# Hybrid GLA, window-attention and PEER block on one core: 19 instead of 14 experts' up-products done beside the gate layout

## The chip, the core and the metric

The kernel is one layer of a diffusion backbone, run on one NeuronCore of a Trainium2 chip. The metric is the device time of the whole kernel in microseconds (us), median over runs. Five engines work side by side, each through its own instructions in the order written: PE (matmuls), DVE (vector), ACT (scalar, activation functions), POOL (GpSimd) and SP, which here only issues transfers. Transfers run on DMA queues and are issued by SP, by ACT (the writes of the gate layout) and by POOL (the gathers).

## What is computed

The first half of the layer (modulation, projections, gated linear attention, window attention, output projection, layer norm) makes a stream `x1` of 1024 tokens. The second half, where the change lies, retrieves for each token 8 heads x 16 of 16384 single-neuron experts:

```python
def _peer(h, peer_wq, peer_subkeys, peer_u, peer_v):
    ...
        top_s, pos = lax.top_k(cand, PEER_TOPK)
        eidx = jnp.take_along_axis(cidx, pos, axis=-1)
        gate = jax.nn.softmax(top_s, axis=-1)
        u = peer_u[eidx]
        v = peer_v[eidx]
        act = jax.nn.gelu(jnp.einsum('pd,phkd->phk', xt, u).astype(jnp.float32), approximate=False)
        return jnp.einsum('phk,phkd->pd', (gate * act).astype(v.dtype), v)
```

All is float32. The kernel gets close to float32 from the faster matmul format by splitting each operand into a high and a low part and adding three products (`mm3`, lines 113 to 117).

## The kernel before, in words

The 1024 tokens are 8 tiles of 128. Five of them (`ND = 5`) go the **dense** way: all 16384 experts are computed for these 640 tokens, and a mostly empty gate matrix selects. Three (`NS = 3`) go the **sparse** way: for each of 3 x 128 (tile, rank) steps one gather fetches the 128 tokens' expert rows (`uv`, 1 MB), DVE makes the dot product, ACT the Gelu, and the weighted value rows are added.

The 16384 experts are 128 rows of 128. The text calls one such row, `jj` = 0 to 127, "an expert" as the change does. One expert's **up-product** (`products`, line 901) is: two loads of 256 KB (`uraw`), their split into `uhi` (ACT) and `ulo` (POOL or DVE), and two halves of 24 matmuls of 128x320 into PSUM (`pact`), 48 matmuls in all. Its **gating** (`gated`, line 1071) is Gelu, times the gate, and a split into `W`. Its **output** (`outputs`, line 1105) multiplies `W` with the value rows; experts go in pairs (`JG = 2`), and each pair ends in ten additions to `yacc` on DVE (line 1120). While the outputs of one pair are computed, the up-products of the next pair are woven in.

The order of the program is this:

- The **gate layout** (`gates`, line 779). For each dense tile it turns the retrieved expert numbers and gates into a matrix `g_d` in DRAM. It goes in 160 steps of four tokens: DVE makes two one-hot tiles (`oa`, line 824, and `wb`, line 810), ACT scales four of them (`ob`, line 828), PE multiplies (`pgb`, line 832), ACT copies the result out (`gstage`, line 834). Every eighth step ACT issues a write to `g_d`.
- Beside its later part run the last pair's retrieval (`rest`), the first 20 sparse steps (`first`), and the up-products of some experts ahead of time (`early`, the table `EARLY`). An early expert's product goes to DRAM (`act_d`, lines 1042 and 1043) and is read back by `gated` when its turn comes. There `ulo` is made by POOL (line 111).
- The **dense stage** then goes over `jj` = 0 to 127. For an expert in `EARLY` it loads `gearly` (160 KB a half) in place of computing the products; for the others it computes them, and makes `ulo` on DVE (line 900). The rest of the sparse steps are spread over it: `advance` counts 0.25 for each half of a product and 0.1 for each of the ten outputs of a pair, and asks for so many sparse steps by the share done.
- At the end come the last pair's outputs and the last layer norm.

Parts that run side by side are interleaved by `weave`, which gives each part a number of steps and a share of the stretch. The lines are:

```python
weave((made, GLEFT, *SPANS[0]), (rest(), 34, *SPANS[1]), (early(), 2 * len(EARLY), *SPANS[2]), (first(), FIRST, *SPANS[3]))
...
made = None if jj in EARLY or jj in filled else products(jj, ep, pe, (7, 2, 2))
```

After `weave` a scheduler still moves instructions of one engine past each other where data allow, so the built order of each engine is what counts. It is shown with the change.

Of the kernel before, what the change touches and what calls it, by code (L numbers as in the profile page):

```python
# [37 lines left out]
def kernel(ctx: ExitStack, tc: tile.TileContext, A, out):  # L38
# [49 lines left out]
    g_d = drm.tile([TD // GT, 128, 128, GT], F32, name="g_d")  # L88
    act_d = [drm.tile([128, TD], F32, name=f"act_d{j}") for j in range(len(EARLY))]

# [4 lines left out]
    def weave(*parts):  # L95

        parts = [(g, n, *(at or (0, 1))) for g, n, *at in parts]
        order = sorted((a + (s + 0.5) / n * (b - a), i) for i, (_, n, a, b) in enumerate(parts) for s in range(n))
        for _, i in order:
            next(parts[i][0], None)  # L100
        for g, *_ in parts:
            for _ in g:
                pass
# [798 lines left out]
    def products(jj, ub, pb, bufs):  # L902

        u = []
        for c in range(2):
            raw = ub.tile([128, 4, 128], F32, tag="raw", name="uraw", bufs=bufs[0])
            nc.sync.dma_start(raw, A["ut"][jj, :, 4 * c:4 * c + 4, :])
            hi = ub.tile([128, 4, 128], F32R, name="uhi", bufs=bufs[1])
            lo = ub.tile([128, 4, 128], F32R, name="ulo", bufs=bufs[1])
            if pb is ps:  # L910
                split(hi, lo, raw, G)
            else:
                apart(hi, lo, raw, "u")
            u.append((hi, lo))
        for h in range(2):
            p = pb.tile([128, 512], F32, tag="trp", name="pact", bufs=bufs[2])
            for k in range(KC):
                mm3(p[:, :HW], [x[:, k % 4, :] for x in u[k // 4]], [x[:, k, HW * h:HW * h + HW] for x in hhD], k, KC)
            yield h, p[:, :HW]
# [115 lines left out]
    with ExitStack() as gx:  # L1035
        ue = pool(gx, "ue", side="right")

        def early():
            for i, jj in enumerate(EARLY):
                for h, p in products(jj, ue, ps, (3, 2, 2)):  # L1040
                    ga = ue.tile([128, HW], F32, name="gact", bufs=2)
                    S.activation(ga, p, AF.Copy)
                    nc.sync.dma_start(act_d[i][:, HW * h:HW * h + HW], ga)
                    yield
# [3 lines left out]
        def first():  # L1048

            for _ in range(FIRST):  # L1050
                next(steps)
                done[0] += 1
                yield

        done = [0]
        def rest():

            yield from after
            retrieved.append(True)

        weave((made, GLEFT, *SPANS[0]), (rest(), 34, *SPANS[1]), (early(), 2 * len(EARLY), *SPANS[2]), (first(), FIRST, *SPANS[3]))
    px.close()
# [9 lines left out]
    def gated(jj, h):  # L1072
# [7 lines left out]
        w = wts[jj]  # L1080
        if jj in EARLY:
            src = ep.tile([128, HW], F32, name="gearly", bufs=2)
            nc.sync.dma_start(src, act_d[EARLY.index(jj)][:, HW * h:HW * h + HW])
        else:
            src = acts.pop((jj, h))
        if jj in EARLY or jj in filled:
            ga = pe.tile([128, 512], F32, tag="trp", name="gact", bufs=2)[:, :HW]
# [86 lines left out]
PICK = 1.3  # L1174
GATE = 1
GLEFT = 152
SPANS = ((0, 1), (0, 0.6), (0.5, 1), (0.2, 0.8))
EARLY = [0, 1, 2, 3] + list(range(12, 128, 12))
UB = 3
BATCH = 2  # L1180
FIRST = 20
# [124 lines left out]
```

## Time and profile before

| what | value |
|---|---|
| time, median of 3 runs | 3144.02 us (3141.66 to 3146.41) |
| the profiled execution's own time | 3149.91 us |
| its span, first to last instruction | 3148.1 us |
| mean granted TensorE clock | 0.948 |
| gate layout, first `gstage` to last | 857.8 to about 1316 us |
| first early product's matmul | 999.0 us |
| last early product's matmul | 1229.6 us |
| first matmul of an output (`pyd`) | 1344.4 us |
| last product's split (`W`) | about 3086 us |

How to read it: busy times of engines overlap, and their sum is no time. In a row of a group "mean ns of one" is the time of one instruction; matmuls are pipelined, so the time from the start of one to the start of the next is shorter than that. The share of each engine over the whole span mixes stages with different limits, so each stage is read by itself.

### The profile page before, as it was taken

The numbers are of one execution on the slowest core, as the hardware profiler recorded it, in microseconds if no ns is written. First come the engines' busy times: TensorE is split into PE (matmuls) and PEld (weight loads), VectorE is DVE, ScalarE is ACT, GpSimd is POOL, SyncE is SP. The second block draws the span as 40 slices with busy tenths as digits, with TensorE's granted clock in tenths as the row PEclk, the third lists the DMA queues.
The fourth block names the chain that finished last, engine by engine and source line by source line (L and its number), as shares of the span: only waits on it lengthen the run. The fifth ranks groups of instructions, "written<-read, shape, count | busy, mean of one in ns | idle before, by whom it ended". The sixth has DMA issues, their size and how long they took to land. (4 is left out here: it accounts for less than half of the span.)

```text
span 3148.1 us, 49158 instructions
## 1 busy us (share of the span) xinstructions
PE 2829.2 (90%) x16604; PEld 2449.8 (78%) x16604; DVE 2349.6 (75%) x5684; ACT 1837.6 (58%) x3947; POOL 1609.1 (51%) x1111
## 2 busy tenths in 40 slices
PE   6998878888778887889999999999999999999994
PEld 3687856767568787768888888888988888989993
DVE  4318844578798999478788877777777778787878
ACT  3324544443546778766666666666666666666673
POOL 0012301043443544137667666767667677777775
PEclk8999879989889999999999999999999999999997
DMA  9653665646466566678799998888988989898983
GB/s 329 222 185 123 211 228 201 211 166 201 153 231 224 218 221 255 254 237 321 288 321 336 335 329 302 314 312 312 345 304 308 324 323 342 330 338 324 340 323 144
DMA packets 352680, 848.82 MB, mean 270 GB/s; under 512 B 27627, under 2 KB 165611, under 8 KB 299692
## 3 DMA queue, kind: packets, MB, share of 16 engines
q1 hardware_dynamic: 285520, 384.20, 37.1%
q0 software_dynamic: 55296, 402.68, 33.6%
q10 hardware_dynamic: 11612, 58.81, 4.8%
q8 instruction: 131, 2.15, 0.3%
q14 instruction: 121, 0.99, 0.1%
HBM read 745.43 MB, written 100.16 MB: 269 GB/s over the span
## 5 line engine op out<-in xcount | busy, mean ns | idle before, releaser
L1023 POOL TENSOR_TENSOR ys<-ys,uv 128x1024 f32<-128x1024 f32 x362 | 870.2, 2404 | 454.0 <-ACT uv L1022 421.2
L117 PE MATMUL pact<-hhD,ulo 128*128 128x320 f32 x2048 | 639.9, 314 | 15.3 <-POOL ulo L111 14.3
L115 PE MATMUL pact<-hhD,uhi 128*128 128x320 f32 x2048 | 641.9, 314 | 10.9 <-DVE W L111 8.2
L116 PE MATMUL pact<-hhD,uhi 128*128 128x320 f32 x2048 | 639.1, 312 | 0.0
L115 PE MATMUL pyd<-vhi,W 128*128 128x512 f32 x1280 | 505.5, 402 | 32.8 <-DVE yacc L1120 22.6
L116 PE MATMUL pyd<-vlo,W 128*128 128x512 f32 x1280 | 508.0, 397 | 18.0 <-DVE vlo L900 17.8
L117 PE MATMUL pyd<-vhi,W 128*128 128x512 f32 x1280 | 506.1, 397 | 0.0
L1120 DVE TENSOR_TENSOR yacc<-yacc,pyd 128x512 f32<-128x512 f32 x630 | 418.6, 681 | 101.1 <-PE pyd L117 100.0
L989 POOL DMA_INDIRECT uv<-in_uv_dram,ex x384 | 375.1, 977 | 222.3 <-issue 53.6
L1006 DVE SCALAR_TENSOR_TENSOR uv<-uv,h2p 128x1024 f32<-128x1024 f32 x384 | 464.1, 1212 | 17.1 <-DMA uv<-in_uv_dram,ex 15.9
L117 PEld LDWEIGHTS pact<-hhD,ulo 128*128 128x128 f32 x2048 | 390.2, 191 | 30.6 <-POOL ulo L111 15.9
L115 PEld LDWEIGHTS pact<-hhD,uhi 128*128 128x128 f32 x2048 | 390.5, 191 | 29.9 <-DVE W L111 10.0
L1022 ACT ACTIVATE uv<-uv,w 128x1024 f32<-128x1024 f32 x362 | 395.3, 1140 | 29.6 <-DVE w L1011 14.3
L116 PEld LDWEIGHTS pact<-hhD,uhi 128*128 128x128 f32 x2048 | 390.5, 191 | 11.7
L115 PEld LDWEIGHTS pyd<-vhi,W 128*128 128x128 f32 x1280 | 242.2, 190 | 86.8 <-DVE yacc L1120 33.3
L116 PEld LDWEIGHTS pyd<-vlo,W 128*128 128x128 f32 x1280 | 243.5, 190 | 60.3 <-DVE vlo L900 20.9
L117 PEld LDWEIGHTS pyd<-vhi,W 128*128 128x128 f32 x1280 | 243.3, 190 | 53.9 <-DVE W L111 0.6
L832 PE MATMUL pgb<-ob,oa 128*128 128x128 f32 x1280 | 196.0, 300 | 56.0 <-ACT ob L828 37.2
L900 DVE TENSOR_TENSOR vlo<-pv,vhi 128x512 fp32r<-128x512 f32 x256 | 175.7, 686 | 93.6 <-ACT pv L899 92.9
L895 ACT ACTIVATE vhi<-vraw 128x512 fp32r<-128x512 f32 x256 | 157.7, 625 | 140.2 <-DMA vraw<-in_uv_dram 94.0
L832 PEld LDWEIGHTS pgb<-ob,oa 128*128 128x128 f32 x1280 | 179.6, 204 | 69.3 <-ACT ob L828 55.7
L828 ACT ACTIVATE ob<-wb,gj 128x128 f32<-128x128 bf16 x640 | 209.5, 409 | 10.6 <-DVE wb L810 7.8
(357 smaller groups left out, 5378.0 us busy)
## 6 DMA issues: line engine op xcount, KB each, us to landing
uraw<-in_ut_dram SPq DMA_DIRECT2D x256, 256.0 KB, 6.7
vraw<-in_uv_dram SPq DMA_DIRECT2D x256, 256.0 KB, 6.8
g_d<-gstage ACTq DMA_DIRECT2D x20, 2048.0 KB, 6.7
gload<-g_d SPq DMA_DIRECT2D x32, 1280.0 KB, 13.8
wo<-wo_d SPq DMA_DIRECT2D x64, 512.0 KB, 5.9
wq<-wq_d SPq DMA_DIRECT2D x64, 512.0 KB, 6.3
wt<-in_w_ada_dram SPq DMA_DIRECT2D x48, 512.0 KB, 5.4
wq_d<-wqs SPq DMA_DIRECT2D x16, 512.0 KB, 6.3
```

The costliest lines, as they stand in the source:

```text
L115: PE.matmul(out_, l[0], r[0], start=(k == 0), stop=False)
L116: PE.matmul(out_, l[0], r[1], start=False, stop=False)
L117: PE.matmul(out_, l[1], r[0], start=False, stop=(k == n - 1))
L828: S.activation(o[1][:, c], w[:, :, c], AF.Copy, scale=gj[:, q + c:q + c + 1])
L832: PE.matmul(p[:, c::4], o[0][:, h + c], o[1][:, h + c], start=True, stop=True)
L895: S.activation(hi, src, AF.Copy)
L900: V.tensor_tensor(lo, p, hi.bitcast(F32), OP.subtract)
L989: G.indirect_dma_start(out=uv[n][0].rearrange("p a d -> p (a d)"), out_offset=None, in_=A["uv"], in_offset=bass.IndirectOffsetOnAxis(ap=ch ...
L1006: pin(V.scalar_tensor_tensor(t[:, 0], t[:, 0], 1.0, h2[j], OP.mult, OP.mult, accum_out=w[:, i:i + 1]))
L1022: S.activation(v, v, AF.Copy, scale=wb)
L1023: G.tensor_tensor(ys[j], ys[j], v, OP.add)
L1120: V.tensor_tensor(ya, ya, p, OP.add)
```

## The change

`EARLY` names 19 experts in place of 14, every eighth from 8 on in place of every twelfth from 12 on, and the early products' share of the woven stretch begins at 0.35 in place of 0.5:

```diff
-SPANS = ((0, 1), (0, 0.6), (0.5, 1), (0.2, 0.8))
-EARLY = [0, 1, 2, 3] + list(range(12, 128, 12))
+SPANS = ((0, 1), (0, 0.6), (0.35, 1), (0.2, 0.8))
+EARLY = [0, 1, 2, 3] + list(range(8, 128, 8))
```

So five experts' products (240 matmuls, 10 loads, 10 `uhi`, 10 `ulo`) leave the dense stage and stand beside the gate layout, with 10 copies `gact` and 10 writes `act_d` more there, and 10 loads `gearly` more in the dense stage. In the dense stage their `ulo` was on DVE, with a copy `pu` on ACT; beside the gate layout it is on POOL.

On **PE**, at the end of the gate layout. `pgb` are the gate layout's matmuls, `pact` those of the up-products. Up to the first of these rows both kernels have the same order of PE from the first `pgb` on. Before:

```order
L116 MATMUL pact<-hhD_10355,uhi 128x320
L117 MATMUL pact<-hhD_10354,ulo 128x320
L832 MATMUL pgb<-ob,oa 128x128 x186
L115 MATMUL pact<-hhD_10354,uhi 128x320
L116 MATMUL pact<-hhD_10355,uhi 128x320
L115 MATMUL pact<-hhD_10354,uhi 128x320
```

Now, a piece of the same stretch and its end:

```order
L832 MATMUL pgb<-ob,oa 128x128 x5
L117 MATMUL pact<-hhD_10359,ulo 128x320
L832 MATMUL pgb<-ob,oa 128x128 x5
L115 MATMUL pact<-hhD_10359,uhi 128x320
L832 MATMUL pgb<-ob,oa 128x128
L116 MATMUL pact<-hhD_10360,uhi 128x320
L832 MATMUL pgb<-ob,oa 128x128 x2
```

```order
L832 MATMUL pgb<-ob,oa 128x128
L116 MATMUL pact<-hhD_10360,uhi 128x320
L117 MATMUL pact<-hhD_10359,ulo 128x320
L832 MATMUL pgb<-ob,oa 128x128 x48
L115 MATMUL pact<-hhD_10359,uhi 128x320
```

The 186 `pgb` that stood alone now have all 240 added `pact` among their first 138; the last 48 stand alone. The `pact` behind the last `pgb` are those of the dense stage's first experts in both.

On **ACT**, in the same stretch (`uhi` and `gact` belong to early products, `w` to a sparse step, the rest to the gate layout). Before:

```order
L1010 ACTIVATE w<-w 128x1
L828 ACTIVATE ob<-wb,gj 128x128 x16
L1010 ACTIVATE w<-w 128x1
L834 ACTIVATE gstage<-pgb 128x128x4
L828 ACTIVATE ob<-wb,gj 128x128 x4
L834 ACTIVATE gstage<-pgb 128x128x4
```

Now:

```order
L1042 ACTIVATE gact<-pact 128x320
L828 ACTIVATE ob<-wb,gj 128x128 x13
L1010 ACTIVATE w<-w 128x1
L828 ACTIVATE ob<-wb,gj 128x128 x3
L1042 ACTIVATE gact<-pact 128x320
L110 ACTIVATE uhi<-uraw 128x512
L834 ACTIVATE gstage<-pgb 128x128x4
L828 ACTIVATE ob<-wb,gj 128x128 x4
```

The ten `uhi` and ten `gact` stand between the gate layout's steps, some right beside the sparse steps' `w`.

On **POOL**, from the last early `ulo` on (`uv` are the gathers). Before:

```order
L735 TENSOR_TENSOR oh<-ohb,ce 128x800 x2
L111 TENSOR_TENSOR ulo<-uraw,uhi 128x512
L735 TENSOR_TENSOR oh<-ohb,ce 128x800
L111 TENSOR_TENSOR ulo<-uraw,uhi 128x512
L989 DMA uv<-in_uv_dram,ex_10021 128x2048 x11
L1023 TENSOR_TENSOR ys<-ys,uv 128x1024 x2
```

Now:

```order
L989 DMA uv<-in_uv_dram,ex_10026 128x2048 x2
L111 TENSOR_TENSOR ulo<-uraw,uhi 128x512 x2
L989 DMA uv<-in_uv_dram,ex_10026 128x2048
L111 TENSOR_TENSOR ulo<-uraw,uhi 128x512
...
L989 DMA uv<-in_uv_dram,ex_10026 128x2048
L111 TENSOR_TENSOR ulo<-uraw,uhi 128x512 x3
L989 DMA uv<-in_uv_dram,ex_10026 128x2048 x3
L1023 TENSOR_TENSOR ys<-ys,uv 128x1024 x2
```

Eight of the eleven gathers now have the ten added `ulo` among and behind them. DVE's instructions in this stretch are the same in number and kind.

## Rows read from the trace of the kernel before

**Rows 1.** Busy share in 40 slices of the span, PE, granted clock, DMA.
```profile
PE   6998878888778887889999999999999999999994
PEclk8999879989889999999999999999999999999997
DMA  9653665646466566678799998888988989898983
```
**Rows 2.** Windows, busy us (instructions) by engine, then clock, DMA share, GB/s.
```profile
1100.00:1225.00 125.00, 104.42 (x726) 101.17 (x725) 120.00 (x233) 100.12 (x285) 61.83 (x53) 0.93 0.59 220
1229.60:1316.50 86.90, 61.94 (x374) 55.16 (x372) 60.05 (x110) 75.40 (x226) 14.73 (x9) 0.92 0.64 250
```
**Rows 3.** Timeline of ACT: start us, us, line, operation, count.
```profile
1299.31 0.60 ACT L834 ACTIVATE gstage<-pgb 128x512 f32<-128x512 f32 x1
1299.79 1.31 ACT L828 ACTIVATE ob<-wb,gj 128x128 f32<-128x128 bf16 x4
1300.99 0.60 ACT L834 ACTIVATE gstage<-pgb 128x512 f32<-128x512 f32 x1
```
**Rows 4.** Waits of ACT, 1229.6 to 1316.5: total us, times, longest.
```profile
ACT w L1010 <- DVE uv L1006: 11.1, 2, 5.7
```
**Rows 5.** Groups of ACT by line, 1000 to 1230: busy us, mean ns, idle before.
```profile
L110 ACT ACTIVATE uhi<-uraw 128x512 fp32r<-128x512 f32 x27 | 16.8, 630 | 3.5 <-PE pact L116 1.9 <-issue 1.5
L1042 ACT ACTIVATE gact<-pact 128x320 f32<-128x320 f32 x28 | 12.0, 434 | 11.9 <-PE pact L117 11.9
```
**Rows 6.** Timeline of PE, `pact` back to back at full clock.
```profile
1325.80 0.31 PE L117 MATMUL pact<-hhD,ulo 128*128 128x320 f32 x1
...
1326.97 0.31 PE L116 MATMUL pact<-hhD,uhi 128*128 128x320 f32 x1
```
**Rows 7.** Windows cut at every tenth `yacc` addition: pairs with one early expert.
```profile
1805.84:1831.86 26.02, 24.04 (x128) 20.70 (x127) 20.54 (x37) 14.25 (x26) 18.85 (x13) 1.00 0.99 362
1980.21:2007.86 27.65, 23.99 (x127) 20.80 (x127) 19.01 (x35) 14.02 (x27) 19.24 (x12) 1.00 0.86 316
2151.45:2178.70 27.25, 24.79 (x124) 21.28 (x123) 19.07 (x37) 14.84 (x27) 17.44 (x11) 0.94 0.92 338
...
2661.99:2682.48 20.49, 20.49 (x112) 18.21 (x111) 17.59 (x34) 13.36 (x23) 13.74 (x9) 1.00 1.03 377
...
sum 234.79, PE 225.97 PEld 198.99 DVE 190.28 ACT 141.02 POOL 158.32; mean PE 22.60 PEld 19.90 DVE 19.03 ACT 14.10 POOL 15.83
```
**Rows 8.** The same cut: the 50 other pairs from 1406.46 to 3061.
```profile
sum 1446.13, PE 1410.31 PEld 1258.92 DVE 1126.13 ACT 954.95 POOL 1032.36; mean PE 28.21 PEld 25.18 DVE 22.52 ACT 19.10 POOL 20.65
```
**Rows 9.** Waits of PE in the dense stage, 1400 to 3084.
```profile
PE pyd L116 <- DVE vlo L900: 17.8, 7, 5.3
PE pyd L115 <- DVE yacc L1120: 16.8, 16, 2.6
PE pact L115 <- DVE W L111: 8.2, 5, 4.5
```
**Rows 10.** Waits of POOL, 1229.6 to 1275.
```profile
POOL uv L989 <- DVE ys L1020: 39.9, 8, 12.1
```
**Rows 11.** Groups of DVE by line, 1100 to 1225.
```profile
L824 DVE TENSOR_TENSOR oa<-iotab,f 128x512 f32<-128x512 bf16 x46 | 37.5, 824 | 0.0
L810 DVE TENSOR_TENSOR wb<-wide,f 128x512 bf16<-128x512 bf16 x47 | 31.0, 666 | 0.0
```
**Rows 12.** The same groups, 1270 to 1316.
```profile
L824 DVE TENSOR_TENSOR oa<-iotab,f 128x512 f32<-128x512 bf16 x26 | 17.9, 690 | 4.1 <-PE pgb L832 2.0
L810 DVE TENSOR_TENSOR wb<-wide,f 128x512 bf16<-128x512 bf16 x22 | 9.3, 424 | 7.9 <-ACT ob L828 7.9
```
**Rows 13.** Groups of POOL by line, 1000 to 1240.
```profile
L111 POOL TENSOR_TENSOR ulo<-uraw,uhi 128x512 fp32r<-128x512 f32 x28 | 39.7, 1425 | 44.4 <-DMA g_d<-gstage 30.1 <-ACT uhi L110 14.2
```
**Rows 14.** DMA issues: count, KB each, median us to landing.
```profile
uraw<-in_ut_dram SPq DMA_DIRECT2D x256, 256.0 KB, 6.7
```

## The prediction, made before the changed kernel was run

> **What bounds the kernel now.** I read the 40 slices first, then windows by stage, then the waits and the timeline of the two stretches that the change touches. The slices [rows 1] show two regimes: from the seventeenth slice on PE is busy at nine tenths at full clock, with DMA at eight or nine tenths; before it PE is at seven or eight. The dense stage is PE's. There PE waits in all for some 43 us of 1684, mostly for DVE: `vlo` late 17.8, `yacc` late 16.8, `W` late 8.2 [rows 9].
>
> The gate layout has two parts. While the retrieval runs beside it (1100 to 1225) DVE is busy 120 of 125 us and is the bound [rows 2]. After the last early product, from 1229.6 to 1316.5, DVE falls to 60 of 86.9 us and ACT is the longest, 75.4 us; it loses 11.1 us more to two waits for a sparse step's dot product, whose gather had not landed [rows 2, 4]. Without these waits a step takes 1.68 us on ACT (four `ob` and one `gstage`, from 1299.31 to 1300.99) [rows 3]. I call this stretch of 86.9 us the tail. PE is busy 61.9 us in it [rows 2], spread out by the waits for `ob`. The built order puts all 240 added matmuls into the tail, and moves nothing ahead of it, although the woven share starts earlier: so the stretch in which DVE is 96% busy keeps its length, and the sum has two terms, the tail and the dense stage.
>
> **The dense stage.** What goes is 5 x 48 matmuls. Back to back at full clock one starts 0.146 us after the other (eight starts in 1.17 us) [rows 6], so an expert is 7.0 us of PE and five are 35.1 us. That is the upper end. The better measure is the pair of experts, since it holds what DVE and DMA take back. Cut at every tenth addition to `yacc`, ten pairs with one early expert took 234.8 us, 23.5 each, and 50 other pairs 1446.1 us, 28.9 each [rows 7, 8]. One product less therefore saved 5.4 us, not 7.0. Five make **27.2 us**; I take this, because the change makes five more of just this kind of pair. What the 1.6 us are: an early pair keeps its ten additions, its `W` and its `vlo`, so DVE is at 190.3 of 234.8 us (81%) against 1126.1 of 1446.1 (78%) [rows 7, 8], and PE catches up with it. With the products ten loads of 256 KB go and ten of 160 KB come; `uhi` and `pu` on ACT and `ulo` on DVE go too. None of these ends last, so I count them at nothing; the cover is PE itself. The sparse steps are paced by the work done, so the same number lies in a shorter stage, about 1.6% denser; the cost of that is in the pair measure only as far as the early pairs already show it. The bound from below is taken from the three worst early pairs, 26.0, 27.7 and 27.3 us [rows 7]: 28.9 less their mean of 27.0 is 1.95, five make 9.8 us.
>
> **The tail.** It gets 240 matmuls on PE (35.1 us), ten `uhi` and ten `gact` on ACT, ten `ulo` on POOL, and on SP ten loads and ten writes.
> - ACT: ten `uhi` and ten `gact` at the busy time of one here, 16.8/27 and 12.0/28 us, are 6.2 + 4.3 = 10.5 us [rows 5]. ACT is the bound, so this is added. Each `gact` also waits for PE's last matmul: 11.9 us over 28 so far [rows 5], ten make 4.3 us. Together **14.8 us**.
> - PE: 61.9 + 35.1 = 97 us must fit into 86.9 + 14.8 = 101.7. It does, with little to spare, and the 61.9 include matmuls drawn out by waits [rows 2], so PE should not end later than ACT. If nothing overlapped, the tail would grow by the full 35.1.
> - POOL: 14.7 us busy [rows 2], plus ten `ulo` at 1.425 us, 14.3 [rows 13]. It has room. But POOL works in order, and eight gathers stand among the `ulo`; see the first rival.
> - SP: the last `act_d` write is now ahead of the six loads for the dense stage's first products. By the built order 32 `ob`, eight steps of 1.68 us or 13.4 us, come after the last `gact`; a load lands in 6.7 us [rows 14]. So I count it at nothing, with 6.7 us to spare.
> - Bounds: below, nothing, if the twenty short ACT instructions fill the 11.1 us in which ACT waits [rows 4]; above, POOL's waits of 39.9 us (first rival). I take 14.8 because ACT's queue is in order: a `gact` behind a waiting `w` waits with it.
>
> DVE's two one-hot instructions show what a busy POOL does beside it: `oa` takes 824 ns and `wb` 666 while POOL is at 61.8 of 125 us, and 690 and 424 when POOL stands still [rows 2, 11, 12]. A step is so 0.376 us dearer for DVE. In the tail POOL would be at 29 of 101.7 us: 46.5 steps x 0.376 x (0.285/0.495) = 10.1 us more on DVE, which has 26.9 us free. I count it at nothing, and it is a rival below. The Trainium skill, "SBUF — State Buffer", section on the two separate sides, states it more sharply: DVE and GpSimd share a port pair as an exclusive lock, and whoever comes second is fully blocked for the whole instruction. The slower `oa` and `wb` agree with that; by this rule all ten `ulo` could stand in DVE's way, 14.3 us by their duration here, and the sum would come to +1.9.
>
> **Sum.** -27.2 + 14.8 = **-12.4 us**. The profiled execution took 3149.9, so its like would take 3137.5; it lies 5.9 above the median of the runs, so I forecast a median of **3131.6 us**. Alone this case reaches from about 3122 to 3140 (tail 8 to 22, dense 22 to 33).
>
> **The rivals.**
> 1. *POOL's gathers hold the added products: slower.* A `ulo` behind a gather waits for whatever the gather waits for: a free buffer, which DVE's `ys` of an older sparse step gives. Over 1229.6 to 1275 POOL waited so 39.9 us in eight waits, the longest 12.1 [rows 10]. If these reach PE through `ulo`, the `pgb` queued behind on PE stand too, and with them ACT's `gstage`. The tail grows by 39.9: -27.2 + 39.9 = +12.7, **3156.7**. It decides from the point where the tail grows by more than 27.2. For it: seven of ten `ulo` stand before the last of the eight gathers. Against it: the eight gathers were all issued by 1275, 45 us into the tail [rows 10], and in the built order 102 of the 186 `pgb` stand ahead of the products of the last three `ulo`; these are 25.5 steps, 43 us at ACT's pace alone. So it is close, but mostly in step. Chance 0.13.
> 2. *The dense stage gives little back.* The stage is already near its transfers' limit: the shortest early pair ran at 377 GB/s and a DMA share of 1.03 [rows 7]. If the added early pairs are like the three worst, 9.8 us come back: +5.0, **3149**. Against it: the ten took 234.8 us, so the other seven average 22.0 [rows 7]. Chance 0.16.
> 3. *The tail swallows the work.* ACT's added 14.8 fill its 11.1 us of waits: +3.7, and -23.5 in all, **3120.5**; with the full 35.1 of the dense stage 3112.6. For it: PE and POOL have room in these waits; against it the order. Chance 0.11.
> 4. *POOL's `ulo` hold DVE, and DVE becomes the tail's bound.* The 10.1 us come on top: -2.3, **3141.7**. Against it are DVE's 26.9 free us. Chance 0.08.
>
> That the change does nothing is no rival: the order shows the 240 matmuls moved.
>
> **Numbers.** My forecast has 0.52. A measurement of this kernel tells 0.2%, 6.3 us, from no change. Faster: 0.42 of the forecast, rival 3, and a little of rival 4: 0.55. Same: 0.10 of the forecast, rival 4, and half of rival 2: 0.25. Slower: rival 1 and the rest of rival 2: 0.20. The range reaches down to rival 3 with the upper bound of the dense stage, and up to most of rival 1: 3113 to 3154; about 0.15 is left out.
>
> **What would show it.** In the profile of the changed kernel: the last `gstage` some 15 us later than 1316, with the first early product still near 999; in the tail ACT still the busiest, near 86 us; `pgb` waiting mainly for `ob`. In the dense stage fifteen early pairs of about 23.5 us, the others at 28.9, and first `pyd` to last some 27 us shorter. If the last `gstage` comes 30 us or more later and PE waits for `ulo` in the tail, rival 1 is right; if early pairs take 26 us or more, or other pairs grow beyond 29.5, rival 2; if the last `gstage` moves less than 6 us, rival 3; if DVE's idle time in the tail is gone and `pgb` waits for `oa`, rival 4. The forecast is wrong if the tail grows by more than 25 us or the dense stage shrinks by less than 18.

## The result: faster by 44 us, with the profile after

| what | before | after |
|---|---|---|
| median of 4 runs (us) | 3144.92 (3141.66 to 3146.41) | 3101.21 (3094.94 to 3112.23) |
| profiled execution's own time, span | 3149.91, 3148.1 | 3094.94, 3093.2 |
| first `pact` / last `gstage` | 999.0 / 1315.8 | 1002.1 / 1325.1 |
| first `pyd` / last `pyd` | 1344.4 / 3105.6 | 1355.9 / 3033.2 |
| last `pyd` to the end | 42.5 | 59.9 |

The ratio is 0.9856, 95% interval 0.9833 to 0.9879. The forecast was 3131.6 (3113 to 3154): the sign held, the size did not. The two profiled executions differ by 54.9 us: the first `pyd` comes 11.5 later, the dense stage is **83.9 shorter** (forecast 27.2), and the end **17.4 longer** (forecast nothing).

**The tail.** The window of the changed kernel that answers to the second of [rows 2], from the last product of the fourteenth early expert to the end of the gate layout:

```profile
1233.20:1326.70 93.50, 84.55 (x614) 80.35 (x613) 65.84 (x109) 84.87 (x247) 25.45 (x20) 1.00 0.71 270
```

Waits of ACT in it, against [rows 4] (total us, times, longest):

```profile
ACT gstage L834 <- PE pgb L832: 2.4, 4, 1.0
ACT uhi L110 <- PE pact L116: 2.4, 2, 1.4
ACT uhi L110 <- DMA uraw<-in_ut_dram: 2.1, 1, 2.1
ACT w L1010 <- DVE uv L1006: 0.6, 1, 0.6
...
ACT gact L1042 <- ACT w L1010: 0.3, 1, 0.3
```

Waits of POOL in it, against [rows 10]:

```profile
POOL uv L989 <- DVE ys L1020: 21.4, 6, 7.7
POOL ulo L111 <- ACT uhi L110: 20.3, 4, 14.8
```

Waits of PE in it:

```profile
PE pgb L832 <- ACT ob L828: 3.5, 11, 0.6
PE pact L117 <- POOL ulo L111: 3.1, 4, 1.3
```

ACT is busy 9.5 us longer (84.87 against 75.40), and the stretch grew by 6.6 us (93.50 against 86.90), so ACT's idle time fell by 2.9 only: its waits for `w` went from 11.1 to 0.6, but others came, for PE (2.4 and 2.4) and for a load (2.1). POOL's waits (a third one, 28.2 us, stands behind the last `ulo`) reach PE for 3.1 us. The runs below repeat the size: from the first `gstage` to the last it is 455.7 to 458.0 us in all eight kernels with 14 experts and 462.1 to 465.9 in all eleven with 19. Of the 11.5 us by which the first `pyd` is later, 3.2 lie ahead of the first `gstage` (857.8 and 861.0), where nothing was changed; over all runs that time lies between 857.8 and 868.3.

**The dense stage.** The whole of it, before and then after:

```profile
1344.39:3105.59 1761.20, 1704.30 (x9166) 1511.01 (x9166) 1381.94 (x2547) 1134.95 (x2011) 1216.82 (x722) 0.99 0.88 316
```

```profile
1355.93:3033.23 1677.30, 1649.22 (x8925) 1470.15 (x8926) 1371.88 (x2527) 1122.23 (x1984) 1209.24 (x719) 0.99 0.91 330
```

Early pairs after, cut as [rows 7]: the fourth, the shortest and the longest of the fifteen, and their sum; then the sum of 44 other pairs, against [rows 8]:

```profile
1740.32:1761.56 21.24, 20.51 (x111) 18.35 (x112) 19.49 (x32) 14.46 (x24) 17.65 (x10) 1.00 0.90 294
...
2166.49:2186.43 19.94, 19.94 (x108) 17.65 (x107) 17.18 (x34) 12.28 (x22) 13.41 (x8) 1.00 1.01 349
...
2377.58:2399.39 21.81, 21.79 (x117) 19.27 (x117) 19.25 (x38) 14.10 (x25) 17.18 (x11) 1.00 1.06 393
...
sum 310.77, PE 310.02 PEld 273.80 DVE 266.54 ACT 198.22 POOL 234.37; mean PE 20.67 PEld 18.25 DVE 17.77 ACT 13.21 POOL 15.62
```

```profile
sum 1263.89, PE 1244.41 PEld 1119.96 DVE 1014.21 ACT 861.03 POOL 915.27; mean PE 28.28 PEld 25.45 DVE 23.05 ACT 19.57 POOL 20.80
```

An early pair takes 20.7 us in place of 23.5, and none of the fifteen is slow; the others take 28.7 in place of 28.9. A pair with one product has 48 `pact` and 60 `pyd`, 108 matmuls; the windows after have x111, x108 and x117, while those of [rows 7] have x128, x127, x124 and x112. What that means for the forecast is said below. Waits of PE from 1400 to 3012, against [rows 9]:

```profile
PE pyd L115 <- DVE yacc L1120: 7.7, 5, 2.9
PE pact L115 <- ACT uhi L895: 6.7, 3, 4.7
PE pyd L116 <- DVE vlo L900: 3.5, 3, 1.5
PE pact L115 <- DVE W L111: 2.3, 1, 2.3
```

**A measure of what PE loses.** Between the first and the last `pyd` one `pact` starts usually 0.147 us after the one before it, one `pyd` 0.231 (medians of the starts). Before there are 5328 and 3837 such distances, or 1670 us; after 5088 and 3837, or 1634. What the stage takes beyond that I call its *stalls*: 92 us before, 43 after. So the 84 us are 35 of matmuls and **49 of stalls**, which the sum of the forecast did not have. Stalls are counted here and below in the one profiled execution of each kernel. Executions of one kernel lie up to 32 us apart (3112 to 3144 in a3), so a few us of stalls tell nothing.

A part of the stalls is TensorE's clock. In the stage before, the granted clock was at its lower level, 1.2 GHz, for 41.0 us in all, and the matmuls started there took 16.5 us beyond the usual distances; after it is 17.0 and 7.7 us. So some 9 of the 49 us lie in stretches at the lower clock, the other 40 at 2.4 GHz.

**Where stalls lie.** Gates come from DRAM by a `gload` of 1.28 MB for four experts, so every second pair has one: a *gate pair*. In the kernel before 55 of the 92 us lie in the 31 gate pairs, 22 in the 30 others, 15 in the first and last. After it is 23, 10 and 10, and the fifteen gate pairs whose first expert is early have -0.4 together. One of the worst pairs before runs from 1915.5 to 1949.2 (33.7 us) and has no early expert. SP's timeline there:

```profile
1908.15 0.33 SPq L1100 DMA_DIRECT2D vraw<-in_uv_dram  x1
1911.82 0.33 SPq L907 DMA_DIRECT2D uraw<-in_ut_dram  x1
1912.79 0.38 SPq L1078 DMA_DIRECT2D gload<-g_d  x1
1916.34 5.91 SPq L907 DMA_DIRECT2D uraw<-in_ut_dram  x1
1922.37 1.15 SPq L1100 DMA_DIRECT2D vraw<-in_uv_dram  x2
```

The pair itself, then the waits of ACT, DVE and PE in it:

```profile
1915.47:1949.21 33.74, 29.04 (x152) 25.27 (x151) 20.93 (x40) 16.69 (x32) 19.00 (x12) 0.95 0.76 273
...
ACT vhi L895 <- DMA vraw<-in_uv_dram: 10.5, 1, 10.5
...
DVE vlo L900 <- ACT pv L899: 7.9, 3, 7.1
...
PE pyd L116 <- DVE vlo L900: 4.7, 1, 4.7
```

Behind the `gload` the issue of the next `uraw` itself takes 5.91 us in place of 0.33. The `vraw` behind it are issued late, and they land late too: the second, issued at 1923.20, took 15.4 us to land where the median is 6.8. ACT waits 10.5 us for one, and the lateness runs on to PE, whose granted clock falls to 1.2 GHz at 1940.0, right behind its wait of 4.7 us. Of the seven waits of PE for `vlo` before, five, with 16.4 of the 17.8 us, come some 2 us after such a wait of ACT for a `vraw`. The same place in an early gate pair of the changed kernel (1847.2 to 1867.9, 20.7 us):

```profile
1840.92 0.33 SPq L1100 DMA_DIRECT2D vraw<-in_uv_dram  x1
1841.29 0.43 SPq L1083 DMA_DIRECT2D gearly<-act_d  x1
1843.72 0.33 SPq L1100 DMA_DIRECT2D vraw<-in_uv_dram  x1
1846.23 0.38 SPq L1078 DMA_DIRECT2D gload<-g_d  x1
1847.21 8.32 SPq L907 DMA_DIRECT2D uraw<-in_ut_dram  x1
```

The issue behind the `gload` is as slow (8.32), but two `vraw` are out ahead of it, and in this pair PE, DVE and ACT wait for no load. The early expert asks for no `uraw`, so the others can be further ahead in their ring: so I read it, but the ring was not tried by itself. SP's issues of over 1 us from 1400 to 3000 are 37 with 213 us before, 40 with 244 us after. So SP is held no less than before; what differs, as I read it, is what stands behind it. Each of the 30 loads that d1 (below) moves to ACT is some 2,576 packets of 509 bytes on average; `uraw` and `vraw` go in packets of 2,048. Whether SP stands for the size of a `gload` or for the number of its pieces was not tried.

**The end.** POOL's last two additions of the sparse steps after; before, the last began at 3079.4, ahead of the last `pyd`:

```profile
3040.61 2.34 POOL L1023 TENSOR_TENSOR ys<-ys,uv 128x1024 f32<-128x1024 f32 x1 [6.95 <-issue]
3045.20 2.34 POOL L1023 TENSOR_TENSOR ys<-ys,uv 128x1024 f32<-128x1024 f32 x1
```

Now they come 7 and 12 us behind the last `pyd`, and the last tile's layer norm with them.

### The profile page after: what moved, and what is told of

It reads as the page before. It is cut to its first block, busy times and chain, and to the rows that moved or that the text cites. A ratio compares the mean times of both kernels' runs of the same rounds, so it can differ in the third digit from the quotient of the medians.

```text
span 3093.2 us, 49192 instructions
## 1 busy us (share of the span) xinstructions
PE 2788.3 (90%) x16604; PEld 2424.9 (78%) x16604; DVE 2351.1 (76%) x5674; ACT 1837.5 (59%) x3947; POOL 1620.8 (52%) x1121
## 5 line engine op out<-in xcount | busy, mean ns | idle before, releaser
L117 PE MATMUL pact<-hhD,ulo 128*128 128x320 f32 x2048 | 641.0, 314 | 20.7 <-POOL ulo L111 20.4
L115 PE MATMUL pact<-hhD,uhi 128*128 128x320 f32 x2048 | 642.7, 314 | 11.5 <-ACT uhi L895 8.7
L115 PE MATMUL pyd<-vhi,W 128*128 128x512 f32 x1280 | 501.2, 398 | 21.0 <-DVE yacc L1120 12.7
L117 PEld LDWEIGHTS pact<-hhD,ulo 128*128 128x128 f32 x2048 | 390.4, 191 | 31.7 <-POOL ulo L111 23.5
L895 ACT ACTIVATE uhi<-uraw 128x512 fp32r<-128x512 f32 x218 | 136.1, 626 | 139.1 <-PE pact L116 137.0
L832 PE MATMUL pgb<-ob,oa 128*128 128x128 f32 x1280 | 186.9, 289 | 33.0 <-ACT ob L828 19.7
```

Of the source, the lines that this page charges most:

```text
L115: PE.matmul(out_, l[0], r[0], start=(k == 0), stop=False)
L117: PE.matmul(out_, l[1], r[0], start=False, stop=(k == n - 1))
L832: PE.matmul(p[:, c::4], o[0][:, h + c], o[1][:, h + c], start=True, stop=True)
L895: S.activation(hi, src, AF.Copy)
```

## Experiments

All runs against the kernel before, four executions each (a3: ten). *Covered* gate pairs are those whose first expert is early, *uncovered* the others, with their count in brackets; "gate pairs" and "others" are stalls in us, "end" is from the last `pyd`.

| run | experts | `gload` | stalls | gate pairs: covered, uncovered | others | end | median | ratio to before, 95% interval |
|---|---|---|---|---|---|---|---|---|
| before | 14 | SP | 92 | 11 (10), 44 (21) | 22 | 42.5 | 3144.9 | |
| after | 19 | SP | 43 | 0 (15), 23 (16) | 10 | 59.9 | 3101.2 | 0.9833-0.9879 |
| a1 | 19 | SP | 39 | 0 (15), 19 (16) | 9 | 59.4 | 3096.0 | 0.9817-0.9868 |
| a2 | 14 late | SP | 70 | 6 (10), 40 (21) | 11 | 42.5 | 3119.8 | 0.9885-0.9939 |
| a3 | 14 early | SP | 75 | 14 (10), 33 (21) | 14 | 41.9 | 3128.5 | 0.992-0.997 |
| a4 | 19, second | SP | 62 | none, 45 (31) | 7 | 60.1 | 3107.4 | 0.9833-0.9896 |
| c3 | 19, other pairs | SP | 61 | none, 50 (31) | 3 | 61.3 | 3116.8 | 0.981-0.9937 |
| b3 | 25 | SP | 47 | 3 (10), 26 (21) | 7 | 96.9 | 3126.7 | 0.9918-0.9951 |
| b4 | 19, `SHARE` 0.94 | SP | 50 | 11 (15), 19 (16) | 10 | 49.2 | 3092.7 | 0.9808-0.9841 |
| b1 | 14 | none | 45 | 3 (10), 7 (21) | 22 | 42.5 | 3106.6 | 0.9855-0.9888 |
| b2 | 19 | none | 46 | 8 (15), 6 (16) | 23 | 42.7 | 3083.9 | 0.9794-0.9827 |
| c1 | 14 | ACT | 37 | 1 (10), 9 (21) | 17 | 42.5 | 3108.4 | 0.9804-0.992 |
| c2 | 19 | ACT | 26 | 0 (15), 5 (16) | 9 | 59.2 | 3094.0 | 0.9762-0.9877 |
| c4 | 19, `SHARE` 0.94 | ACT | 29 | 1 (15), 6 (16) | 9 | 49.1 | 3086.9 | 0.9735-0.9852 |
| d1 | 14 | mixed | 53 | 4 (10), 13 (21) | 23 | 42.8 | 3115.0 | 0.9868-0.992 |
| d2 | 19 | mixed | 23 | -1 (15), 5 (16) | 8 | 58.6 | 3072.4 | 0.9733-0.9776 |
| d3 | 19, `SHARE` 0.94 | mixed | 35 | 1 (15), 6 (16) | 19 | 49.1 | 3080.2 | 0.9753-0.9797 |
| e1 | 19, other pairs | mixed | 28 | none, 16 (31) | 2 | 61.6 | 3085.1 | 0.9762-0.9828 |
| e2 | 14 early | mixed | 41 | 2 (10), 6 (21) | 18 | 42.5 | 3098.8 | 0.981-0.9881 |
| e3 | 14 late | mixed | 31 | 2 (10), 5 (21) | 11 | 42.7 | 3091.4 | 0.9787-0.985 |

### Number, spacing or chance: four tables of early experts

The changed kernel's `SPANS` put back (a1); then other tables, with `SPANS` as changed:

```diff
-SPANS = ((0, 1), (0, 0.6), (0.35, 1), (0.2, 0.8))
+SPANS = ((0, 1), (0, 0.6), (0.5, 1), (0.2, 0.8))
-EARLY = [0, 1, 2, 3] + list(range(8, 128, 8))
+EARLY = [0, 1, 2, 3] + list(range(48, 128, 8))   # a2
+EARLY = [0, 1, 2, 3] + list(range(8, 88, 8))     # a3
+EARLY = [0, 1, 2, 3] + list(range(9, 128, 8))    # a4
```

a1: 

> The change with its second edit undone: 19 experts at every eighth place, but the early products' share begins at 0.5 again. All theories of the dense stage expect the time of the changed kernel, about 3101 us (within 6), and a dense stage (first to last pyd) near 1677 us, since PE's order beside the gate layout is the same with either value. If the share's beginning is what brought the gain, it comes out near 3145.

a2: 

> 14 experts as before, but every eighth from 48 on (0 to 3, then 48, 56, ... 120) in place of every twelfth. Theory 1 (only the number counts: each expert moved takes about 17 us off the dense stage, from 1761 to 1677 for five, wherever it stands): a dense stage of about 1761 and 3145 us in all. Theory 2 (an early pair every fourth pair lets DVE, ACT and the transfers catch up, so that the pairs between lose their stalls): the part from 48 on runs like the changed kernel's, early pairs near 20.7 us, the part ahead of it like the kernel's before without early pairs, 28.9 a pair; dense stage about 1715 to 1735. Theory 3 (chance: each table gives another order, and each order falls differently against the gathers and loads): anything from 1690 to 1780, in no relation to the spacing.

a3: 

> 14 experts as before, every eighth from 8 to 80 in place of every twelfth. Theory 1 (only the number counts): a dense stage of about 1761 us and 3145 in all. Theory 2 (close early pairs take the stalls away): early pairs near 20.7 us in the first two thirds, 28.9 a pair in the last third, dense stage about 1715 to 1735. Theory 3 (chance of the order): anything from 1690 to 1780, and not the same as 14 experts placed late.

a4: 

> The change with its places moved by one: 0 to 3, then 9, 17, ... 121; the same pairs hold an early expert, but as their second member. Theories 1 and 2 (number; spacing): as the changed kernel, about 3101 us (within 8), dense stage 1677, early pairs 20.7 us. Theory 3 (chance of the order): the dense stage differs by 20 us or more from 1677, toward 1734 (1761 less the forecast 27).

The second edit of the change does nothing that can be told (3096.0). The number alone does not explain the gain: a2 and a3 have 14 experts as before and are faster, 0.9912 and 0.9945. Against spacing alone there is only a hint: a4 has the changed kernel's pairs, and 62 us of stalls in its profiled execution. But that was the slowest of a4's four (3113.4), as the changed kernel's was the fastest of its four (3094.9), a4's median of 3107.4 lies within the 8 us that the spacing theory allowed, and its dense stage is 19 us longer, where chance was to show by 20. What a4 had lost, if anything, is that there the early expert is the second of its pair: its gate pairs have 45 us of stalls again.

### The gate loads left out, and issued by ACT

```diff
-        if jj % GJ == 0 and h == 0:
+        if jj % GJ == 0 and h == 0 and jj < 8:          # b1 (before), b2 (after)
```

b1: 

> The kernel before, without 30 of its 32 loads of the gates (gload, 1.28 MB each, 38 MB of about 556 MB that the dense stage moves): the experts from 8 on are all gated by the first gates that were loaded, so this part of the computation is left out. PE's starts of before in the dense stage add up to 1761 us, of which 92 are gaps beyond the usual distance of two starts (stalls); the changed kernel has 43, the changed kernel with the old share 39, 14 experts placed late or early 70 and 75, 19 experts at odd places 62. Theory A (the stalls come from transfers that land late, and moved experts help because they ease the transfers): stalls fall from 92 to under 50 and the time to about 3100 us. Theory B (the stalls come from how each built order happens to place work on the engines): stalls stay at 80 or more, the time within 10 us of 3146.

b2: 

> The changed kernel, without the same 30 loads of the gates (that part of the computation is left out). Theory A: the stalls of 43 us fall to about 20, so the distance between the two kernels without these loads shrinks toward the 35 us of matmuls less what stands in the tail (about 20 to 25 us in all). Theory B: stalls stay near 43, and the distance to the kernel before without these loads stays near 45 us.

Theory A held for b1: stalls fall from 92 to 45, the time by 40 us. In b2 A expected 20 us of stalls; the gate pairs' fall from 23 to 14, but those of the other pairs grow from 10 to 23, and the sum stays at 46 (the 17 us that b2 is faster than the changed kernel lie at its end). The medians are 22.8 apart, in A's 20 to 25. Without these loads the dense stages are 1714.9 and 1679.9 us: 35.0 apart, the 240 matmuls and nothing else. But bytes left out may act as bytes. So the same loads were issued by ACT:

```diff
-            nc.sync.dma_start(loads[0].rearrange("p a j t -> p a (j t)"),
+            nc.scalar.dma_start(loads[0].rearrange("p a j t -> p a (j t)"),   # c1 (before), c2 (after), c4 (after, SHARE = 0.94)
```

c1: 

> The kernel before, with the loads of the gates (gload) issued by ACT in place of SP; no byte less is moved. In the kernel before, SP's issues of the next loads stand behind a gload: 37 issues of over 1 us, 212.6 us in all, against 2 issues and 2.6 us without the gate loads. Theory A1 (the stalls of transfers come from SP's queue, where a 256 KB load stands behind the 1.28 MB): SP's long issues go, ACT's waits for vraw fall from 89 to under 30 us, stalls fall from 92 to 45 to 55 and the time to 3100 to 3112, about as without the gate loads. Theory A2 (they come from the bytes): stalls stay near 90 and the time within 8 us of 3146. If ACT is held by its own issue, the time may even grow.

c2: 

> The changed kernel with the loads of the gates issued by ACT. Theory A1 (early experts at every eighth place stand right where a gate load is, and have taken its stalls away already): little is left to gain; stalls stay at 40 to 50 and the time near 3095 (3088 to 3103), and the distance to the kernel before with the same edit shrinks to 10 to 20 us. Theory A2 (bytes): the time as the changed kernel's, and the distance to the kernel before with the same edit stays near 45.

The view of the loads `vraw` from 1400 to 3000 (name, count: shortest/median/longest issue in ns) and ACT's wait for them. Before:

```profile
L1100 SPq DMA_DIRECT2D vraw<-in_uv_dram x229: 327/328/11457, 1402.4 to 2998.7; - x115
...
  DMA vraw<-in_uv_dram: 89.1, 26
```

Without the gate loads (b1):

```profile
L1100 SPq DMA_DIRECT2D vraw<-in_uv_dram x235: 327/328/333, 1408.0 to 2999.4; - x118
...
  DMA vraw<-in_uv_dram: 10.9, 11
```

With all but the first two on ACT (d1, below), where the same bytes move:

```profile
L1100 SPq DMA_DIRECT2D vraw<-in_uv_dram x233: 327/328/448, 1406.4 to 2990.0; - x117
...
  DMA vraw<-in_uv_dram: 24.4, 15
```

So the stalls of the gate pairs come from `gload` standing in SP's queue, not from its bytes: the long issues are gone, and c1 takes 3108.4 with 37 us of stalls, fewer than the 45 to 55 of A1, while its transfers run at a DMA share of 0.91 and 328 GB/s, no less than before (0.88 and 316). A2 is out. c2 gains 7 us only, as A1 said, and lies 14.4 from c1 (10 to 20 expected), but its stalls fell to 26 where 40 to 50 had been expected.

### The early experts put beside no gate load

```diff
-EARLY = [0, 1, 2, 3] + list(range(8, 128, 8))
+EARLY = [0, 1, 2, 3] + list(range(10, 128, 8))   # c3; e1 with the mixed gate loads
```

c3: 

> 19 experts in the same distance, but at 10, 18, ... 122 in place of 8, 16, ... 120, so that every early expert of the dense stage stands in a pair that has no gate load; gate loads come with every fourth expert. In the kernel before 55 of its 92 us of stalls lie in the pairs during which a gate load's experts are computed, in the changed kernel those of its early pairs have none (-0.4 against 24.3 at the same places). Theory A1 (an early expert beside a gate load hides it): stalls come back to 65 to 75, dense stage about 1700 to 1710, time about 3120. If only the number counts: stalls near 45, dense stage about 1680, time 3101.

Measured 61 us of stalls, a dense stage of 1695.5 and 3116.8, each a little under what A1 said and far from the other. The gate pairs of c3, all 31, and those of the kernel before without an early expert, 21:

```profile
sum 908.33, PE 878.37 PEld 780.39 DVE 703.45 ACT 598.88 POOL 624.50; mean PE 28.33 PEld 25.17 DVE 22.69 ACT 19.32 POOL 20.15
```

```profile
sum 618.49, PE 592.05 PEld 526.51 DVE 457.27 ACT 389.47 POOL 424.33; mean PE 28.19 PEld 25.07 DVE 21.77 ACT 18.55 POOL 20.21
```

A gate pair takes 29.3 and 29.5 us there; in the kernel d1, where the same 21 pairs add up to 585.03, 27.9. Over all runs an uncovered gate pair stalls 1.2 to 2.1 us with `gload` on SP, 0.2 to 0.6 with it on ACT or left out; a covered one -0.03 in the changed kernel, up to 1.4 elsewhere. So an early expert beside the load does not always hide it: in a3 the ten covered pairs stall 1.4 each and the uncovered ones 1.6, and in b4, with the changed kernel's table, it is 0.7 and 1.2. What lets the covered pairs escape in the changed kernel is not shown.

### The first two gate loads back on SP

With all of them on ACT the first `pyd` comes 17 us (c1) and 12 us (c2) later. The mixed form leaves the first two on SP:

```diff
+            (nc.sync if jj < 8 else nc.scalar).dma_start(loads[0].rearrange("p a j t -> p a (j t)"),   # d1 (before), d2 (after), d3 (after, SHARE = 0.94), e1 to e3
```

d1: 

> The kernel before with the first two gate loads on SP as they were, and the other thirty issued by ACT. With all on ACT the stalls fell from 92 to 36 us, but the first pyd came 16.7 us later (1361.05 against 1344.4), because the first two loads then stand in ACT's order. Theory A1 with this reading: first pyd back near 1345 to 1348, stalls 36 to 45, time 3092 to 3100. If the delay of the first pyd is not the gate loads', the time stays near 3108.

d2: 

> The changed kernel with the same edit. First pyd back from 1367.5 to about 1356 to 1358, stalls 26 to 35, the stretch behind the last pyd still near 59 us; time 3080 to 3090. The distance to the kernel before with this edit is what the change is worth where no load stands behind a gate load: 35.3 us of matmuls, plus 0 to 10 of stalls, less about 9 beside the gate layout and 17 at the end: 9 to 20 us, near the 12.4 that had been forecast.

d2 is the fastest kernel of all, **3072.4 us**, 0.9754 of before. Its first `pyd` is back at 1354.4, about as expected, and ACT waits 6.5 us for `vraw` from 1400 to 3000. Its time is 8 us below the range expected, and its stalls are 23 in place of 26 to 35. d1 missed the other way: the first `pyd` is back at 1348.5, but with 53 us of stalls it takes 3115.0, 6.6 more than c1 with all loads on ACT. So the two are 42.6 us apart where 9 to 20 were expected. 14 of the 29 us that d1 stalls longer lie in pairs without a gate load (22.5 against 8.1). Hence three more:

e1: 

> 19 experts at 10, 18, ... 122 (pairs without a gate load), with the gate loads from the third on issued by ACT. With the loads on SP these places had 61 us of stalls against 43 of the changed kernel's places. Theory A1 (the places mattered only through the gate loads on SP): both now have about the same, 23 to 33 us, and the time is 3072 to 3082. If the places matter in another way: stalls 40 or more, 3090 or more.

e2 (the table of a3): 

> 14 experts, every eighth from 8 to 80, with the later gate loads issued by ACT. The kernel before with this edit has 52.6 us of stalls and 3115 us, the changed kernel with it 23.2 and 3072. Theory N (the rest of the stalls falls with the number of early experts, 14 or 19): 45 to 60 us of stalls, 3107 to 3120. Theory O (it is the built order that each table gives): anywhere from 20 to 55, and so 3085 to 3117.

e3 (the table of a2): 

> 14 experts, every eighth from 48 to 120, with the later gate loads issued by ACT. Theory N: 45 to 60 us of stalls, 3107 to 3120, the same as with 14 placed early. Theory O: anywhere from 20 to 55, 3085 to 3117, and not the same as 14 placed early.

e1's stalls speak for A1: with the loads on SP these places had 61 us against 43, with the later ones on ACT 28 against 23. Its time does not say it as plainly: 3085.1, 3 above A1's range and 12.7 above d2, where the same two tables were 15.6 apart with the loads on SP. Of the 17 us between the profiled executions of e1 and d2, 8 lie ahead of the first `gstage` (868.3 and 860.1), where nothing differs, and 5 in the dense stage, which was 18 longer in c3 than in the changed kernel. e2 and e3 have 41 and 31 us: theory N is out. Theory O is what is left; its ranges were wide, and what in the order does it is not known. d2 is 26 and 19 us faster than these two: the 35 us of matmuls less the 6.6 of the tail and the 17.4 of the end make 11, and the stalls differ by 18 and 8. What decides the stalls of 2 to 23 us in the pairs without a gate load was not found.

### More experts, and the end

```diff
+EARLY = [0, 1, 2, 3] + list(range(6, 128, 6))   # b3
+SHARE = 0.94                                     # b4, c4, d3; it was 0.98
```

b3: 

> 25 experts, every sixth from 6 on. If each expert more takes its 7.05 us of matmuls off the dense stage and some 3 us of stalls, six more shorten it from 1677 to about 1615 to 1635; if the stalls are chance, to 1635 plus or minus 20. The tail beside the gate layout has no waits of ACT left to fill (0.6 us for the sparse steps), and PE was busy for 84.6 of about 93.5 us; so each added expert now costs it its full 7 us: six make it 42 us longer, and the time is near 3101 (within 15).

b4: 

> The changed kernel with its sparse steps asked for earlier (done by 0.94 of the dense stage's work in place of 0.98). In the changed kernel the last 17 us are lost behind the last matmul, because the sparse steps lag: the last dot product stands behind all 640 additions to yacc. If that lag is the cause, the stretch from the last pyd to the end shrinks from 59.9 to about 43 us and the time by 10 to 17 us, to about 3088; if the denser sparse steps only delay PE in their place, the dense stage grows by as much and the time stays near 3101.

c4: 

> The changed kernel with the gate loads issued by ACT and the sparse steps done by 0.94 of the work: stalls of 40 to 50 and the stretch behind the last pyd at 43 to 49 us in place of 59.9, so about 3083 to 3093, a little faster than either edit alone. If the transfers set the pace of the sparse steps, nothing is added to the better of the two.

d3: 

> The changed kernel with the same edit and the sparse steps done by 0.94 of the work: the stretch behind the last pyd near 49 us, first pyd near 1357; time 3072 to 3082, the fastest of all.

b3 missed by 25 us. Its last `gstage` came 31.8 us later than in the changed kernel (42 expected), and its dense stage was 1639.1 us, 38.2 shorter. That is the six experts' 42 us of matmuls less 4 us by which the stalls grew (47 against 43), and above the 1615 to 1635 that three us of stalls an expert would have made. So there is hardly a gain, and the end, 96.9 us, takes it: its last gather was issued at 3061, 30 us behind the last `pyd` (3030.8). The end is 42 to 43 us in all kernels with 14 experts, 59 to 62 with 19 and the old `SHARE`, 97 with 25, and 42.7 again with 19 when the gate loads' 38 MB are left out (b2). So the sparse steps lag where the same gathers have to fit into a shorter stage; that transfers hold them rests on b2 alone. Asking for them earlier takes the end to 49 in b4, c4 and d3, where 43 was hoped for in b4. In b4 and c4 that is a gain of 8.5 and 7.1 us over the same kernel without it (10 to 17 expected for b4, which is 3.3 below a1); in d3 stalls grow by 12 us, and it is slower than d2 by 8, where it was expected to be the fastest.

## Why the prediction was wrong

- **The dense term (27.2) is the step that failed**; 83.9 was measured. It has two faults, and the second is the larger.
  - "One product less therefore saved 5.4 us, not 7.0" compared the means of [rows 7] and [rows 8]. But a window cut at DVE's additions does not hold the matmuls of its own pair alone: the ten early windows held 65.3 `pact` and 54.4 `pyd` each, not 48 and 60, the fifty others 92.5 and 61.1. At 0.147 and 0.231 us these are 22.2 of 23.5 us and 27.7 of 28.9, so a pair of either kind stalled alike (1.3 and 1.2 us), and the missing 1.6 us were matmuls of neighbours, not what "DVE and DMA take back". The matmuls give back their full 7.05 us: 35.0 between b1 and b2, whose stalls are the same. That is the upper end (35.1), which I had and set aside.
  - Beside it 49 us of stalls went, which the sum put at nothing. Of these 32 lay in gate pairs, 12 in the other pairs, 5 in the first and last. That `gload` on SP makes the stalls of the gate pairs is shown (b1, c1, d1), and c3 shows that they come back when no early expert stands first in one. (In a3 the covered pairs stall nearly as much as the others, so this is not the whole condition.) Some 22 of the 32 lay in pairs that are covered now: 11 of the ten that were covered already, 11 of the five new ones. The other 10 went from sixteen uncovered pairs, which stall 1.4 in place of 2.1 each. For these, for the 12 and the 5, the cause stays open.
- The three slow early pairs, which I used as a bound from below, were gate pairs with 2.7 to 4.9 us of stalls in them.
- **"Ten loads of 256 KB go and ten of 160 KB come ... None of these ends last, so I count them at nothing."** Wrong in the place, not in the bytes: I followed no single pair's queue on SP. [rows 9] had the sign: `vlo` late by 17.8 us in seven waits, the largest of PE's waits. I read it as DVE's, where 16.4 of it follow a `vraw` that landed late. Without the gate loads (b1) PE waits 0.5 us for `vlo`.
- **The tail (14.8)**: 6.6. ACT's added busy time was right (9.5 against 10.5). That each `gact` waits for PE was wrong: no such wait is left in the tail, where 4.3 us were forecast. That ACT's waits stay was half wrong: 11.1 for `w` went to 0.6, and 6.9 new ones came. So rival 3's mechanism is there in part, between its own 3.7 and my 14.8; by the sign set for it (last `gstage` less than 6 us later) it is not met, as that came 9.3 later, and its time of 3112.6 missed for the stalls and the end. PE was busy 84.6 us where 97 had been summed, at a granted clock of 1.00 against 0.92 in the tail before.
- **Rival 1** (POOL's gathers hold the products): the waits are there, 21.4 and 20.3 us, but PE waits only 3.1 us for `ulo`: the products stayed in step with the gate layout, as argued.
- **Rival 2** (the dense stage gives little back): its sign, early pairs of 26 us or more, did not come; the longest is 21.8.
- **Rival 4** (DVE is held by POOL): in the tail `oa` went from 688 to 756 ns and `wb` from 420 to 535, 7.1 us more busy time on DVE beside 13.6 us of `ulo`, where 10.1 had been estimated. DVE had the room. By the rule that I had cited from the Trainium skill ("SBUF — State Buffer", section on the two separate sides: whoever comes second is blocked for the whole instruction) it could have been all of the 13.6; about half of that is seen, so the trace does not contradict it.
- **The end**: I named no cost, although I saw that the sparse steps lie denser. It took 17.4 us back.
- The sign held, as both terms had it right; that the tail cost less than forecast and the end more is no merit of the sum.
- The profiled executions differ by 54.9 us, the medians by 43.7: the one before lay 5.0 above its median, the one after 6.3 below. So some 11 us of the terms above, most likely of the stalls, belong to these two executions and not to the kernels; which, is not shown.
- In [rows 1] PE reaches nine tenths from the nineteenth slice on, not the seventeenth; no term hangs on it.

## What to carry to other kernels

A mean over windows holds whatever falls into them, neighbours' work and stalls too: before multiplying it, count the bounding engine's instructions in each window, split the time into its pace and the rest, and ask of each slow stretch which transfer was in front of the late one. A large load in a queue of small ones can delay them by more than its bytes, since the issues behind it stand (37 issues, 213 us of SP here). Giving it another issuer took 39 us off the kernel before (c1). Leaving the loads that the first work waits for where they are gave 22 us more in the changed kernel (d2 against c2), but in the kernel before it cost 7 (d1 against c1): try both. And where a stage gets shorter, look which side work is paced by it: here it came out at the end.

## What the runs showed of the hardware

- An issue on SP, 0.33 us as a rule, took up to 11.46 us behind a 1.28 MB load in the kernel before and up to 14.2 in the changed one, longer than a 256 KB load takes to land (6.8 us, median). From ACT the same load was issued in 0.37 us, and SP's issues of `vraw` then took 0.45 us at most (d1). The Trainium skill, "DMA: Bandwidth & Descriptors", section "Issuing engines are not separate DMA queues", says that issuing from several engines "will only save the time on the sequencer it takes to initiate the DMA, which is usually small relative to the DMA itself". That time is not small here: 213 us of SP in one stage, and c1 is 39 us faster than the kernel before on the same chip. Whether it is all that was saved no run here shows, since on ACT the loads also go through another queue (q10 in place of q1).
- 14 experts with the later gate loads on ACT, in the orders that three tables give, stall between 31 and 53 us (d1, e2, e3) and take 3091 to 3115 us, a spread larger than most of the terms of the forecast.
